# A two-layer hybrid trunk on one Trainium2 core: prologue in four quarters of channels, and five smaller edits

## The chip, the core and the metric

The kernel runs on one core of a Trainium2 chip. The engines are TensorE (PE; its weight loads are listed apart as PEld), VectorE (DVE), ScalarE (ACT), GpSimd (POOL) and SyncE (SP), which issues nearly all transfers. The metric is the device time of one execution in microseconds. TensorE has two clock levels, 1.2 and 2.4 GHz; the profile gives the granted clock as a share of full speed (0.50 and 1.00).

## What is computed

Two layers over 256 latent and 256 context tokens of width 1024, and a last norm of the latent tokens:

```python
for l in range(DEPTH):                                    # DEPTH = 2
    mod = silu_c @ mod_w[l] + mod_b[l]                    # 6 x 1024 values: shift, scale, gate, twice
    mod_c = silu_cc @ mod_w[l] + mod_b[l]
    ...
    h = rms_norm(x, norm_mix_g[l]) * (1.0 + sc1) + sh1    # the same for the context, with mod_c
    p = h @ w_in[l]
    # four mixers on column groups of p, in both directions: RG-LRU, RWKV-7, mLSTM, gated DeltaNet;
    # the context's final states start the latent tokens
    x = x + gt1 * (jnp.concatenate([ya, yb, yc, yd], axis=-1) @ w_out[l])
    h2 = rms_norm(x, norm_ffn_g[l]) * (1.0 + sc2) + sh2
    # layer 0: dense SwiGLU (2816 wide); layer 1: top 2 of 8 experts (1408 wide), latent tokens only
    y = swiglu(...) if l % 2 == 0 else moe_swiglu(...)
    x = x + gt2 * y
return rms_norm(x, final_norm_g)
```

## The kernel before

**Layout.** Activations lie as [128 channels x 512 tokens] tiles, eight to the width; columns 0 to 255 are context, 256 to 511 latent. Weights come from HBM as fp32 and are split on the fly by `wsplit` (lines 249 to 263): ACT casts a high part `whi` (L260), DVE subtracts to get the rest, `wlo` (L262). The normed activation is split in the same way into `hh` and `hl`. `mm3` then makes three matmuls of each product: hh by whi, hl by whi, hh by wlo. Nearly every matmul goes through the helper `mm` and shows line 246.

**Prologue** (`run`, lines 2157 to 2186). SP issues the constants `cst` (L197, 772 KB), the vectors of both layers (L200), the eight tiles of x (L2173), and 16 tiles `mw` of 512 KB with the modulation weights of shift and scale of layer 0's first norm. ACT and DVE add up the squares of x (`stat_add`, L376 to 380), `rms_rows` turns them into a row of factors `rs` in PSUM. `mod_block(0, j, True)` (L290 to 321) makes shift (j = 0) and scale (j = 1): 32 matmuls each with the two condition vectors as the 32-column stationary side, a copy to SBUF (`msb`), two transposes (L314), and the bias add into `mod`. Only then `norm` (L396 to 416) makes `nga` (gain times 1 + scale) and the eight normed tiles, and `inproj` (L419 to 446) starts.

**In-projection and loop.** The first group of `inproj` takes 4 output tiles at once, 8 weight tiles k by 12 matmuls, into two `pj` and two `pc` accumulators, and yields after each k. `mixers` (from L1495) runs a loop: each pass takes one step of the projection, and adds a credit to three lanes of mixer work and to the remaining `mod_block`s (in which the weights come in 256 KB tiles). The credits come from a table `PACE` by the number of the projection's step: for layer 0 (16, (1, .96, .6, 0)), then (29, (1.5, 2.4, .45, .5)), and so on to step 54. So the order on each engine follows from the count of yields. `rglru` (from L1430) multiplies by two 64x64 heads at a time, laid on the diagonal of a zero-filled 128x128 stationary tile `lruw`.

**Experts** (`moe_block`, from L1904). Pairs of experts gather their tokens by matmul with a one-hot tile `oh`: 8 tiles of PSUM, cast by ACT to `xgh` and `xgl` (L1960 to 1963). The way back uses the transposed `oht`; for the small experts the 64 rows of the upper and lower half are contracted apart (64 partitions). After the last pair `last_sums` (L1891 to 1902) squares each of the eight result tiles on ACT and sums it over channels by two matmuls with a column of ones (`lsq` in the profile).

**End of run.** All engines read the flag `big` (L2257). Under `tc.If(big > 0)` (L2260) stands the code for experts that overflow their first slots (`moe_rest`, not run with these inputs); `final` (L2129 to 2143) stands behind it.

Of the kernel before, what the change touches and what calls it, by code (L numbers as in the profile page):

```python
# [20 lines left out]
P = 128  # L21
# [44 lines left out]
COLMAP = _colmap()  # L66
T_WA, T_MISC, T_RKV, T_GDN, T_ML, T_LRU = 0, 1, 2, 8, 16, 24
# [20 lines left out]
def _consts():  # L88
# [16 lines left out]
    strict = np.stack([q[:, None] < i[None], q[:, None] > i[None]], 1)  # L105
    incl = np.stack([q[:, None] <= i[None], q[:, None] >= i[None]], 1)
    add("mstrict", strict)
    add("mincl", incl)
    add("id16", np.arange(32)[None, None, :] == 2 * np.arange(16)[None, :, None] + ((p % 32) // 16)[:, None, None])
    t = np.arange(T)  # L110
    rm = np.ones((P, T))
    for r in range(32):
        c = 128 if r < 4 else 64
        rm[r] = (t % c != 0)
        rm[32 + r] = (t % c != c - 1)
    add("rmask", rm)
# [31 lines left out]

def _negmasks():
# [5 lines left out]
    return np.concatenate([g.reshape(P, -1), m.reshape(P, -1)], 1).astype(np.float32)  # L155
# [27 lines left out]
class Trunk:  # L183
    def __init__(self, ctx, tc, t, dbg=None):
# [12 lines left out]
        nc.sync.dma_start(self.cst, t["cst"])  # L197
        self.pvt = [self.cp.tile([P, NPV], F32, name=f"pv{l}") for l in range(L)]
        for l in range(L):
            nc.sync.dma_start(self.pvt[l], t["pv"][l])  # L200
# [5 lines left out]
        nc.scalar.copy(self.identr, self.ident)  # L206

        self.pick = self.cp.tile([P, 2, 10, 64], F32R, name="pick")
        for d in range(2):
# [11 lines left out]
    def k(self, name):  # L221
        o, n = CSTN[name]
        return self.cst[:, o:o + n]
# [171 lines left out]
    def norm(self, l, gname, isc, ish, lo, rs, h32=None):  # L395
# [8 lines left out]
        for k in range(8):  # L404
            t = self.wk.tile([P, 512], F32, name=self.nm("nt"), tag="nt", bufs=3)
            nc.vector.tensor_tensor(t[:, lo:512], self.xT[:, k, lo:512], rs[:, lo:512], op=ALU.mult)  # L406
            for s in range(lo // 256, 2):
                o = t[:, 256 * s:256 * s + 256]
                ga, sh = gas[s][:, k:k + 1], self.modc(l, ish, s, k)
                if s == 0 and k % 2:  # L410
                    nc.vector.tensor_scalar(o, o, ga, sh, op0=ALU.mult, op1=ALU.add)
                else:
                    nc.scalar.activation(o if h32 is None else h32[:, k], o, AF.Identity, scale=ga, bias=sh)
            if h32 is None:
                nc.scalar.copy(self.hh[:, k, lo:512], t[:, lo:512])
                nc.vector.tensor_sub(self.hl[:, k, lo:512], t[:, lo:512], self.hh[:, k, lo:512].bitcast(F32))


    def inproj(self, l, tiles, evac, lat_only=()):  # L419
        if sorted(tiles[0:4]) == list(range(4)):  # L420
            pss = [self.pjt() for _ in range(2)] + [self.ps(), self.ps()]
            for k in range(8):
                wh, wl = self.wsplit(self.t["w_in0"][l, :, k], 4, P)
                for i in range(4):
                    tl, lo = tiles[i], 256 if i in lat_only else 0
                    self.mm3(pss[i][:, lo:512], wh[:, tl], wl[:, tl], self.hh[:, k, lo:512], self.hl[:, k, lo:512],
                             k == 0, k == 7)
                if k < 7:
                    yield
# [19 lines left out]
    def layer_params(self, l):  # L449
        nc = self.nc  # L450
        A = {}
        lw = self.cp.tile([P, 8, P], F32, name=f"lruw{l}", tag="lruw", bufs=1)
# [980 lines left out]
    def rglru(self, l, s, p, state, skip, new):  # L1433
# [64 lines left out]
    def mixers(self, l, xsrc, xdst):  # L1498
# [105 lines left out]
        def proj():  # L1604
            units = dict(rwkv=(0, [7, 6, 0, 1, 2, 3, 4, 5], ev_rwkv, (0, 1, 7), self.rwkv, ((), ())),
# [166 lines left out]
    def moe_route(self):  # L1772
# [20 lines left out]
        gt, eq = one("cgt", (P, 2, 8, 8)), one("ceq", (P, 2, 8, 8))  # L1793
# [97 lines left out]
    def last_sums(self, ms):  # L1891

        nc = self.nc
        for m in ms:
            if m == 0:
                self.lsum = self.ps2(0)
            sq = self.mp.tile([P, 256], F32, name=self.nm("lsq"), tag="hs", bufs=2)
            nc.scalar.activation(sq, self.xT[:, m, 256:512], AF.Square)
            for b in range(2):
                self.mm(self.lsum[:, b, 0:1], sq[:, 128 * b:128 * b + 128], self.one, m == 0, m == 7)  # L1900
            if m == 7:
                nc.vector.tensor_copy(self.ssq, self.lsum[:, :, 0])

    def moe_block(self, ids, cols, small, place, gate, off, last=False):  # L1904
# [8 lines left out]
        if off:  # L1913
            io = T_("ceq", (P, 128), 1)
            nc.vector.tensor_scalar(io, iota, float(off), None, op0=ALU.add)
            iota = io
# [15 lines left out]
        def gather(p):  # L1932
# [16 lines left out]
            for k in range(8):  # L1949
                ps = self.ps()  # L1950
                ohc = lambda b, o, n: cat(oh, 256 * b + o, [[1, n]])
                tk = lambda i, b: (self.tokh, self.tokl)[i][:, b, 128 * k:128 * k + 128]
                for b in range(2):
                    self.mm(ps[:, 0:n], tk(0, b), ohc(b, 0, n), b == 0, b == 1 and not half)
# [440 lines left out]
```

## Time and profile before

| | us |
|---|---|
| median of 3 runs (lowest, highest) | 1874.96 (1871.52, 1887.96) |
| the profiled execution | 1870.76 |
| its span | 1869.0 |
| prologue and the first group of layer 0 (up to 66 us) | 66 |
| rest of layer 0's mixers (66 to 560 us) | 494 |
| dense feed-forward of layer 0 (560 to 940 us) | 380 |
| mixers of layer 1 and router (940 to 1440 us) | 500 |
| experts (1440 to 1843 us) | 403 |
| sums and last norm (from 1843 us) | 26 |

The stages were cut where the lines of the program change. The table of windows gives, per stage, TensorE's busy time and its granted clock; a stage in which the engine is nearly always busy can only get shorter by fewer or faster matmuls, one in which it idles by what it waits for.

### The profile page before, as it was taken

To read this page: it belongs to the slowest core of one execution; us is meant where nothing else is said; L and a number is where in the kernel's file an instruction comes from. 1 tells how busy PE (TensorE), PEld (TensorE's weight loads), DVE (VectorE), ACT (ScalarE), POOL (GpSimd) and SP (SyncE) were. 2 spreads that over 40 slices of the span, in tenths; PEclk is the share of its full clock that TensorE was granted. 3 is DMA by queue.
4 is the path that set the end of the run, shared out by engine and by line. 5 is a ranking of instruction groups with operands and counts; after the bars stand their busy time and mean duration, and the time that the engine had idled before them with its cause. 6 is when DMAs were issued, how large, how long until landed. Compare 5 with 4: busy or idle time off the path is not lost. (4 is left out here: it accounts for less than half of the span.)

```text
span 1869.0 us, 31932 instructions
## 1 busy us (share of the span) xinstructions
PE 1695.7 (91%) x12340; PEld 1301.5 (70%) x12340; DVE 1106.6 (59%) x2414; ACT 901.3 (48%) x1655; POOL 33.5 (2%) x88
## 2 busy tenths in 40 slices
PE   5989988997996999999979899899787999999996
PEld 2767666774784888888867576587676888666663
DVE  5577368778566333333356657787755887364542
ACT  4554464775534333332245545568434776344431
POOL 0000001000000000000000000000000000000000
PEclk8979897998997999999989799899785999999997
DMA  7433343144443333333334344421233998897992
GB/s 283 149 102 130 123 130 108 60 144 162 143 132 101 98 96 96 96 96 96 99 116 149 110 146 159 151 83 62 65 105 124 395 359 286 314 400 291 403 346 118
DMA packets 124002, 309.60 MB, mean 166 GB/s; under 512 B 13440, under 2 KB 39296, under 8 KB 111424
## 3 DMA queue, kind: packets, MB, share of 16 engines
q1 hardware_dynamic: 123840, 307.46, 47.7%
q8 instruction: 99, 1.62, 0.4%
q14 instruction: 63, 0.52, 0.1%
HBM read 286.77 MB, written 20.64 MB: 164 GB/s over the span
## 5 line engine op out<-in xcount | busy, mean ns | idle before, releaser
L262 DVE TENSOR_TENSOR wlo<-w,whi 128x512 fp32r<-128x512 f32 (+3 forms) x386 | 381.4, 993 | 319.7 <-ACT whi L260 305.0
L260 ACT CAST whi<-w 128x512 fp32r<-128x512 f32 (+3 forms) x386 | 332.3, 865 | 397.8 <-PE pj L246 146.1
L246 PE MATMUL pj<-hh,whi 128*128 128x512 f32 (+1 forms) x544 | 225.2, 415 | 29.1 <-ACT whi L260 15.1
L246 PE MATMUL pj<-hh,wlo 128*128 128x512 f32 (+1 forms) x544 | 220.3, 406 | 4.4 <-DVE wlo L262 4.2
L246 PE MATMUL pj<-hl,whi 128*128 128x512 f32 (+1 forms) x544 | 216.8, 399 | 0.4 <-DVE hl L1291 0.2
L246 PEld LDWEIGHTS pj<-hh,whi 128*128 128x128 f32 x544 | 113.1, 208 | 56.9 <-ACT whi L260 19.4
L246 PE MATMUL pj<-mw,sc 128*32 128x256 f32 x768 | 104.0, 428 | 45.4 <-DMA mw<-in_mod_w 45.2
L246 PEld LDWEIGHTS pj<-hh,wlo 128*128 128x128 f32 x544 | 113.3, 208 | 33.9 <-DVE wlo L262 10.1
L246 PEld LDWEIGHTS pj<-hl,whi 128*128 128x128 f32 x544 | 113.7, 209 | 17.6 <-DVE hl L1291 0.9
L246 PE MATMUL pm<-wlo,xgh 128*128 128x512 f32 (+1 forms) x240 | 93.2, 388 | 1.4 <-DVE wlo L262 1.4
L246 PE MATMUL pm<-whi,xgh 128*128 128x512 f32 (+1 forms) x240 | 92.7, 388 | 0.0
L246 PE MATMUL pm<-whi,xgl 128*128 128x512 f32 (+1 forms) x240 | 91.6, 382 | 0.0
L246 PEld LDWEIGHTS pj<-mw,sc 128*32 128x32 f32 x768 | 27.6, 116 | 87.0 <-DMA mw<-in_mod_w 44.4
L246 PE MATMUL pj<-fh,whi 128*128 128x512 f32 x176 | 68.7, 390 | 0.0
L246 PE MATMUL pj<-fh,wlo 128*128 128x512 f32 x176 | 68.6, 390 | 0.0
L246 PE MATMUL pj<-fl,whi 128*128 128x512 f32 x176 | 68.5, 389 | 0.0
L246 PE MATMUL pm<-hh,whi 128*128 128x512 f32 x160 | 62.3, 390 | 0.0
L246 PE MATMUL pm<-hl,whi 128*128 128x512 f32 x160 | 62.3, 389 | 0.0
L246 PE MATMUL pm<-hh,wlo 128*128 128x512 f32 x160 | 62.3, 389 | 0.0
L246 PE MATMUL pm<-w,xgs 128*64 128x192 f32 (+1 forms) x384 | 60.7, 462 | 0.0
L246 PE MATMUL pc<-hh,whi 128*128 128x512 f32 (+1 forms) x128 | 49.6, 387 | 7.5 <-DVE nt L406 4.0
L246 PEld LDWEIGHTS pm<-wlo,xgh 128*128 128x128 f32 x240 | 46.4, 193 | 10.6 <-DVE wlo L262 3.3
(658 smaller groups left out, 3407.2 us busy)
## 6 DMA issues: line engine op xcount, KB each, us to landing
w<-in_moe_gu SPq DMA_DIRECT2D x64, 1024.0 KB, 7.1
mw<-in_mod_w SPq DMA_DIRECT2D x160, 256.0 KB, 3.0
w<-in_moe_d SPq DMA_DIRECT2D x32, 1024.0 KB, 7.6
w<-in_w_in SPq DMA_DIRECT2D x112, 256.0 KB, 2.9
w<-in_moe_gv SPq DMA_DIRECT2D x32, 768.0 KB, 6.2
w<-in_ffn_gu SPq DMA_DIRECT2D x88, 256.0 KB, 2.7
w<-in_moe_d SPq DMA_DIRECT2D x16, 768.0 KB, 6.4
pp<-pd SPq DMA_DIRECT2D x46, 256.0 KB, 3.5
```

Source lines behind the costliest of these rows:

```text
L246: self.nc.tensor.matmul(out, lhsT, rhs, start=start, stop=stop)
L260: nc.scalar.copy(hi, w)
L262: nc.vector.tensor_sub(lo, w, hi.bitcast(F32))
```

## The change

1. **Prologue by quarters.** `first_norm` makes shift and scale for 256 channels at a time: 32 matmuls of 128 columns, one copy (`mqs`), one transpose, bias add and `nga` for two tiles, the norm of these two tiles, and the first group's matmuls for these two k (`inproj_first`). The same 8 MB of modulation weights come in 8 transfers of 1 MB. The first group's accumulators are two `pj` and the two halves of a `pm` pair. `cst` is smaller (266 KB) and is issued behind four of the tiles of x. The first group no longer yields in layer 0, so that the loop has 7 steps fewer before it; `PACE` stays.
2. **Compact masks.** The four masks move from `cst` to `cstm` (192 KB before, 720 KB now) and are kept as bf16 (`maskb`). `lruw` holds 64 columns instead of 128 (no zeros), and `rglru` makes two 64x64 matmuls where it made one of 128x128.
3. **Paired gather.** Four pairs of PSUM tiles (`pm`), with casts of twice the size, in place of eight single ones.
4. **128-row ways back.** A small expert's `oht` is split into two tiles with 64 zero rows each (POOL clears them), and the way back contracts over 128 rows.
5. **Paired squares.** Two squares are added on DVE before the sum, so that `lsq` has 8 matmuls instead of 16, issued one tile later.
6. **Last norm inside the branch.** `If(big < 1)` holds `final` as the way that falls through; `Else` holds the overflow code and a `final` of its own.

```diff
+    def constants(self):
+        nc = self.nc
         nc.scalar.copy(self.identr, self.ident)
+        nc.vector.tensor_copy(self.identb, self.ident)
...
+    def first_norm(self):
+        nc = self.nc
+        rs = None
+        tiles = [self.WTILE[i] for i in RWKV_TILES[0:4]]
+        ps2 = self.ps2(0)
+        self.begun = [self.pjt(), self.pjt(), ps2[:, 0], ps2[:, 1]]
+        m, o = self.modt[0], PVN["modb"][0]
+        gas = [self.sm((P, 8), "nga", 2) for _ in range(2)]
+        for q in range(4):
+            w = [self.wk.tile([P, 4, 512], F32, name=self.nm("mq"), tag="mq", bufs=8) for _ in range(2)]
+            for i in range(2):
+                nc.sync.dma_start(w[i], self.t["mod_q"][q, :, 4 * i:4 * i + 4])
+            if rs is None:
+                rs = self.rms_rows(0)
+            pm = self.ps2(1)
+            for k in range(8):
+                for g in range(4):
+                    self.mm(pm[32 * g:32 * g + 32, 0, 0:128], self.sc[:, k, :], w[k // 4][:, k % 4, 128 * g:128 * g + 128],
+                            k == 0, k == 7)
+            sb = self.wk.tile([P, 128], F32, name=self.nm("mqs"), tag="mqs", bufs=2)
+            nc.vector.tensor_copy(sb, pm[:, 0, 0:128])
+            nc.tensor.transpose(pm[:, 1, 0:128], sb, self.ident)
+            nc.vector.tensor_tensor(cat(m, 4 * q, [[16, 2], [2, 2], [1, 2]]), cat(pm, 512, [[64, 2], [32, 2], [1, 2]]),
+                                    cat(self.pvt[0], o + 2 * q, [[8, 2], [1, 2], [0, 2]]), op=ALU.add)
+            ks = range(2 * q, 2 * q + 2)
+            for s in range(2):
+                nc.vector.scalar_tensor_tensor(gas[s][:, 2 * q:2 * q + 2], cat(m, 16 + 4 * q + s, [[2, 2]]), 1.0,
+                                               self.pv(0, "nmg", 2 * q, 2), op0=ALU.add, op1=ALU.mult)
+            for k in ks:
+                self.norm_tile(0, 0, 0, rs, gas, k)
+            for k in ks:
+                self.inproj_first(0, tiles, (), self.begun, k)
...
     def inproj(self, l, tiles, evac, lat_only=()):
         if sorted(tiles[0:4]) == list(range(4)):
...
+            pss, self.begun = self.begun, None
+            if pss is None:
+                pss = [self.pjt() for _ in range(2)] + [self.ps(), self.ps()]
+                for k in range(8):
+                    self.inproj_first(l, tiles, lat_only, pss, k)
+                    if k < 7:
+                        yield
...
-                self.mm(pp[:, 0, c], A["lruw"][:, 4 * d + j], u[:, j])
-                self.mm(pp[:, 1, c], A["lruw"][:, 4 * d + 2 + j], u[:, j])
+                for g in range(2):
+                    for h in (slice(0, 64), slice(64, 128)):
+                        self.mm(pp[h, g, c], A["lruw"][h, 4 * d + 2 * g + j], u[h, j])
...
+    def last_squares(self, m):
...
+        for h in range(2):
+            nc.scalar.activation(sq[:, h], self.xT[:, m + 4 * h, 256:512], AF.Square)
+        nc.vector.tensor_tensor(sq[:, 0], sq[:, 0], sq[:, 1], op=ALU.add)
...
-            for k in range(8):
-                ps = self.ps()
+            for k2 in range(0, 8, 2):
+                ps = self.ps2()
...
+                nc.scalar.copy(xh[:, k2:k2 + 2, 0:m], ps[:, :, 0:m])
+                nc.scalar.copy(xl[:, k2:k2 + 2, 0:m], ps[:, :, 256:256 + m])
...
+                if small[e]:
+
+                    oht[e] = [T_("oht", (P, 256), 6, F32R) for _ in range(2)]
+                    for h in range(2):
+                        nc.gpsimd.memset(oht[e][h][H_[1 - h]].bitcast(F32), 0.0)
+                        nc.scalar.copy(v2(oht[e][h])[H_[h]], way[H_[h]])
...
         for k in range(8):
+            if k == 4:
+                nc.sync.dma_start(self.cst, self.t["cst"])
+                nc.sync.dma_start(self.pvt[0], self.t["pv"][0])
             nc.sync.dma_start(self.xT[:, k], self.t["x_t"][:, k])
             self.stat_add(k, 0)
...
+        self.constants()
+        self.first_norm()
+        nc.sync.dma_start(self.pvt[1], self.t["pv"][1])
         cm = self.ptile("cstm", (P, CSTM.shape[1]))
...
+        nc.vector.tensor_copy(self.maskb, cm[:, 384:])
...
-        with tc.If(big > 0):
+        with tc.If(big < 1) as here:
+            self.final()
+        with here.Else():
             self.moe_rest()
-            self.last_sums(range(8))
-        self.final()
+            for m in range(4):
+                self.last_squares(m)
+                self.last_sums(m)
+            self.final()
```

What the change moves on the engines is shown at three places. A row is a line of the program, the operation, output <- inputs, and the shape; numbers behind a name tell tiles of one name apart.

The first is TensorE between the modulation and the first group. Before, `mw` are modulation weights, `msb` the copied result, `hh` and `hl` the normed activation:

```order
L246 MATMUL pj_235<-mw_278,sc 32x256 x4
L314 MATMUL pj_286<-cst,msb_284 128x128 x2
L246 MATMUL pj_411<-hh,whi_416 128x512
L246 MATMUL pj_411<-hl,whi_416 128x512
L246 MATMUL pj_412<-hh,whi_416 128x512
```

And in the changed kernel, from the end of the first quarter's matmuls to the start of the second's (`mq` are modulation weights, `mqs` the copied result, pm_280 the second quarter's accumulator, pm_371 the third's):

```order
L264 MATMUL pm_145<-hh,wlo_260 128x512
L264 MATMUL pm_280<-mq_276,sc 32x128 x7
L264 MATMUL pm_280<-mq_277,sc 32x128 x16
L463 MATMUL pm_280<-cst,mqs_313 128x128
L264 MATMUL pm_371<-mq_367,sc 32x128 x16
L264 MATMUL pj_146<-hh,whi_332 128x512
L264 MATMUL pj_147<-hh,whi_332 128x512
```

The modulation of the second quarter, 23 of its matmuls and the transpose, stands behind all of the first quarter's projection; the third and fourth quarter's transposes stand in the same way behind the k tiles of the quarter before.

The second place is VectorE ahead of the last quarter (`maskb` and its neighbours are the masks, `wlo` a split weight, `mod` and `nga` the last quarter's modulation, `lmz` and `lmq` small constants of a mixer):

```order
L438 TENSOR_TENSOR hl<-nt_416,hh 128x512
L462 COPY mqs_495<-pm_462 128x128
L428 TENSOR_TENSOR nt_507<-xT_89,pc_180 128x512
...
L2259 CAST gmaskb<-cstm_550 128x128
L2260 CAST mmaskb<-cstm_550 128x256
L2261 CAST maskb<-cstm_550 128x1024
L280 TENSOR_TENSOR wlo_515<-w_513,whi_514 128x512
...
L464 TENSOR_TENSOR mod_101<-pm_462,pv_70 128x2x4
L468 SCALAR_TENSOR_TENSOR nga_148<-mod_101,pv_70 128x2
```

The casts of the masks, which wait for the transfer of `cstm`, now stand ahead of the last quarter's `mod`; before, the first stood ahead of the second half's copy `msb` and the second behind it, both ahead of the norm.

The third is TensorE at the end. Before (`oht` the way back, `lsq` the squares; the rows behind the branch are the overflow code):

```order
L246 MATMUL pc_16886<-oht_16095,hh 128x256 x2
L246 MATMUL pm_16844<-cst,lsq_16881 128x1 x2
L246 MATMUL pm_16844<-cst,lsq_16893 128x1 x2
L246 MATMUL pm_16844<-cst,lsq_16897 128x1 x2
L2257 TENSOR_LOAD bigi
L2260 COMPARE_AND_BRANCH
L246 MATMUL pc_16921<-oh_16914,hl 128x256 x4
```

And in the changed kernel:

```order
L264 MATMUL pc_16930<-oht_16092,hh 128x256 x2
L264 MATMUL pm_16906<-cst,lsq_16925 128x1 x2
L264 MATMUL pm_16906<-cst,lsq_16939 128x1 x2
L2335 TENSOR_LOAD bigi
L2338 COMPARE_AND_BRANCH
L264 MATMUL pc_16968<-identr,pth_16964 128x128
```

The sum's matmuls are half as many, and directly behind the branch stand the matmuls of the last norm, in which `pth` is the high part of the norm's factors.

## Rows read from the trace of the kernel before

**Rows 1.** The page: busy time, share of the span and instructions of two engines
```profile
PE 1695.7 (91%) x12340; PEld 1301.5 (70%) x12340; DVE 1106.6 (59%) x2414; ACT 901.3 (48%) x1655; POOL 33.5 (2%) x88
```

**Rows 2.** Windows by stage, TensorE: window, length, busy (records), clock, DMA share, GB/s
```profile
0.00:66.00 66.00, 42.83 (x244) 0.90 0.64 237
66.00:560.00 494.00, 454.78 (x4290) 0.90 0.39 126
...
1440.00:1843.00 403.00, 388.11 (x1961) 0.97 0.88 339
1843.00:1869.00 26.00, 11.61 (x52) 0.58 0.12 44
```

**Rows 3.** Timeline of the prologue: start, duration, engine, line, tiles, [idle before <- releaser]
```profile
21.22 1.88 DVE L406 TENSOR_TENSOR nt<-xT,pc 128x512 f32<-128x512 f32 x3 [1.86 <-PE pc L246]
...
26.12 1.50 PE L246 MATMUL pj<-mw,sc 128*32 128x256 f32 x24
...
33.54 1.08 PE L246 MATMUL pj<-mw,sc 128*32 128x256 f32 x8 [0.16 <-DMA mw<-in_mod_w]
...
34.69 0.42 DVE L311 COPY msb<-pj 128x256 f32<-128x256 f32 x1 [0.48 <-PE pj L246]
...
36.30 1.58 ACT L413 ACTIVATE nt<-nt,mod,nga 128x256 f32<-128x256 f32 x3 [17.14 <-DVE nga L402]
...
38.82 1.09 ACT L413 ACTIVATE nt<-nt,mod,nga 128x256 f32<-128x256 f32 x2
...
40.32 0.61 ACT L415 CAST hh<-nt 128x512 fp32r<-128x512 f32 x1
...
40.47 0.79 PE L246 MATMUL pj<-hh,whi 128*128 128x512 f32 x1 [4.61 <-ACT whi L260]
...
41.76 0.69 DVE L262 TENSOR_TENSOR wlo<-w,whi 128x512 fp32r<-128x512 f32 x1
```

**Rows 4.** Timeline, near the end of the first group
```profile
59.78 0.39 PE L246 MATMUL pj<-hl,whi 128*128 128x512 f32 x1
...
64.76 0.39 PE L246 MATMUL pc<-hh,wlo 128*128 128x512 f32 x1
```

**Rows 5.** Windows of 2 us, TensorE, columns as in rows 2
```profile
30.00:32.00 2.00, 0.64 (x8) 0.87 1.02 404
32.00:34.00 2.00, 1.54 (x16) 0.50 1.02 404
...
44.00:46.00 2.00, 2.00 (x8) 0.72 0.22 73
...
66.00:68.00 2.00, 0.90 (x4) 1.00 0.00 0
```

**Rows 6.** Waits of TensorE, 66 to 560 us: us in total, times, longest
```profile
PE pj L246 <- DMA mw<-in_mod_w: 19.4, 16, 3.1
```

**Rows 7.** Groups by shape, whole span: records | busy us, mean ns | idle before, releasers
```profile
L246 PE MATMUL pm<-w,xgs 128*64 128x512 f32 x192 | 44.0, 594 | 0.0
...
L246 PE MATMUL pm<-pp,lruw 128*128 128x256 f32 x64 | 18.3, 413 | 1.6 <-ACT dmb L1452 1.3 <-ACT dgf L1190 0.2
L246 PE MATMUL pc<-oht,hh 128*128 128x256 f32 x80 | 16.9, 314 | 3.9 <-DVE xT L1993 3.5 <-ACT hth L2096 0.4
L246 PE MATMUL pc<-oht,hh 64*128 64x256 f32 x48 | 12.8, 377 | 2.7 <-ACT hh L2101 1.7 <-DVE xT L1993 0.6
```

**Rows 8.** Timeline of the first gather of experts
```profile
1443.76 0.37 ACT L1960 CAST xgh<-pc 128x256 fp32r<-128x256 f32 x1 [1.36 <-PE pc L246]
```

**Rows 9.** Timeline of the end: last squares and sums, branch, last norm
```profile
1844.99 0.61 PE L246 MATMUL pm<-cst,lsq 128*128 128x1 f32 x4
...
1851.55 2.72 PE L246 MATMUL pm<-cst,lsq 128*128 128x1 f32 x12
...
1854.30 0.16 DVE L1902 COPY ssq<-pm 128x2 f32<-128x2 f32 x1 [2.16 <-PE pm L246]
1858.65 0.17 DVE L343 TENSOR_SCALAR rq<-ssq 128x2 f32<-128x2 f32 x1 [4.19 <-DVEq L2260]
```

More of the change, by code (lines that the diff above doesn't have):

```diff
@@ L146, with _masks @@
 CST = _consts()
+MSKN = {}
+def _masks():
+    cols, off = [], 0
+    p = np.arange(P)
+    q, i = p % 64, np.arange(64)
+    t = np.arange(T)
+    rm = np.ones((P, T))
+    for r in range(32):
+        c = 128 if r < 4 else 64
+        rm[r] = (t % c != 0)
+        rm[32 + r] = (t % c != c - 1)
+    for name, a in (("mstrict", np.stack([q[:, None] < i[None], q[:, None] > i[None]], 1)),
+                    ("mincl", np.stack([q[:, None] <= i[None], q[:, None] >= i[None]], 1)),
+                    ("id16", np.arange(32)[None, None, :] == 2 * np.arange(16)[None, :, None] + ((p % 32) // 16)[:, None, None]),
+                    ("rmask", rm)):
+        a = np.asarray(a, np.float32).reshape(P, -1)
+        MSKN[name] = (off, a.shape[1])
+        cols.append(a)
+        off += a.shape[1]
+    return np.concatenate(cols, 1)
 def _negmasks():
@@ L404, in norm @@
         for k in range(8):
[L405 to L413, printed above, removed]
@@ L419, in inproj, with inproj_first @@
+    def inproj_first(self, l, tiles, lat_only, pss, k):
+        wh, wl = self.wsplit(self.t["w_in0"][l, :, k], 4, P)
+        for i in range(4):
+            tl, lo = tiles[i], 256 if i in lat_only else 0
+            self.mm3(pss[i][:, lo:512], wh[:, tl], wl[:, tl], self.hh[:, k, lo:512], self.hl[:, k, lo:512],
+                     k == 0, k == 7)
     def inproj(self, l, tiles, evac, lat_only=()):
         if sorted(tiles[0:4]) == list(range(4)):
-            pss = [self.pjt() for _ in range(2)] + [self.ps(), self.ps()]
@@ L451, in layer_params @@
         A = {}
-        lw = self.cp.tile([P, 8, P], F32, name=f"lruw{l}", tag="lruw", bufs=1)
+        lw = self.cp.tile([P, 8, 64], F32, name=f"lruw{l}", tag="lruw", bufs=1)
         nc.sync.dma_start(lw, self.t["lru_w"][l])
@@ L1889, in moe_main, with last_sums @@
         self.moe_block([ids[s] for s in order], order, [s >= FULL for s in order], self.slot, self.slotg, 0, True)
-    def last_sums(self, ms):
+    def last_squares(self, m):
         nc = self.nc
[L1894 to L1902, printed above, removed]
+        sq = self.mp.tile([P, 2, 256], F32, name=self.nm("lsq"), tag="hs", bufs=2)
+        for h in range(2):
+            nc.scalar.activation(sq[:, h], self.xT[:, m + 4 * h, 256:512], AF.Square)
+        nc.vector.tensor_tensor(sq[:, 0], sq[:, 0], sq[:, 1], op=ALU.add)
+        self.lsq = sq
+    def last_sums(self, m):
+        if m == 0:
+            self.lsum = self.ps2(0)
+        for b in range(2):
+            self.mm(self.lsum[:, b, 0:1], self.lsq[:, 0, 128 * b:128 * b + 128], self.one, m == 0, m == 3)
+        if m == 3:
+            self.nc.vector.tensor_copy(self.ssq, self.lsum[:, :, 0])
     def moe_block(self, ids, cols, small, place, gate, off, last=False):
@@ L1981, in back @@
                 ps = [self.ps(), self.ps()]
[L1982 to L1990 removed]
+                for h in range(2):
+                    for i, e in enumerate(es):
+                        c = 128 * (m if small[e] else m + 4 * h)
+                        for q in range(2):
+                            self.mm(ps[h][:, 0:256], ys[e][q][:, c:c + 128], oht[e][h], i + q == 0, i == len(es) - 1 and q == 1)
+                if sums and m:
+                    self.last_sums(m - 1)
                 for h in range(2):
```

110 lines of the change are left out of this document (46 added, 64 removed).

## The prediction

> **What bounds the kernel now.** I read the page first, then the windows by stage, then the timeline where a stage idles. TensorE is busy for 91% of the span, DVE for 59% [rows 1], so what counts is TensorE's own time and what it waits for. The windows [rows 2] part the span. From 66 to 560 us it idles for 494.00 - 454.78 = 39.2 us, at a granted clock of 0.90; in the experts it is busy for 388.11 of 403 us at 0.97; in the prologue it idles for 23.2 of 66 us, and in the tail for 14.4 of 26 us. The last two are what the change mainly addresses: at most 38 us, 2% of the time.
>
> The prologue in order [rows 3]: from 21.22 the norm's products `nt` are made, and wait; the last modulation matmuls run at 33.54 behind the last `mw` transfer; then comes a chain without cover, the copy at 34.69, the scaling at 36.30, and the first projection matmul at 40.47. The group then runs to about 65.15 (64.76 + 0.39) [rows 4]: 24.7 us for its 96 matmuls. The clock stands at half speed by 33 us and comes back at about 45 us [rows 5]: at 0.72 over 44 to 46 us, about 0.9 of these 2 us ran at full speed. So the group's first 4.6 us ran at half speed, which lost 2.3 us.
>
> **The prologue by quarters.** TensorE executes its rows in order, and the order listed above puts the rest of quarter q's modulation behind the projection of quarter q-1. So the quarters don't overlap; each pays a chain in the open.
>
> - Start. Ahead of x stand 506 KB of constants less (and one `pv`). At the 404 GB/s of a window in which transfers ran without a pause [rows 5] the 506 KB are 1.25 us; with the second `pv` I take 1.7 us (0 to 3), so `nt` starts at 19.5 instead of 21.22. Three products 1.9 [rows 3]: 21.4. From the copy to the scaling the old chain took 36.30 - 34.69 = 1.6: 23.0. Two `wlo` of 0.69 now stand between on DVE: 24.4. Two scalings 1.1 and the cast of `hh` 0.6 [rows 3]: the first matmul is at 26.1 instead of 40.47. The first quarter's modulation has its data well before: 2 MB at 404 GB/s are 5.2 us.
> - Group. Its own 24.7 us stay.
> - Second quarter in the open: 23 modulation matmuls of 128 columns. With 256 columns one took 1.50/24 = 0.063 at full and 1.08/8 = 0.135 at half clock [rows 3]; 23 are 1.4 to 3.1, I take 2.0. Then 1.6 + 1.1 + 0.6 and a handover, 3.4. Sum 5.4.
> - Third: 15 matmuls (0.9 to 2.0, I take 1.2) and 3.4: 4.6. The matmuls issued ahead for the quarter after lie in the chain's shadow.
> - Fourth: its modulation is complete, only its transpose stands behind k tile 5; without the copy, 3.1.
> - The casts of the masks ahead of the last `mod` on DVE wait for `cstm`. It is asked for behind the weights of k tile 7, which need a buffer that k tile 4 frees, around 43 us by these sums; 720 KB then take 1.8 us at 404 GB/s. The last quarter's chain starts near 54: covered by 9 us. Without that cover it would be late by what the transfer is late.
>
> Sum: 26.1 + 24.7 + 5.4 + 4.6 + 3.1 = 63.9, against 65.15: -1.2. On the other side stands the clock. The chains are pauses; around a 2-us pause at 66 us it stayed at full speed, in the gappy 30 to 34 us it fell [rows 5]. Three pauses of 3.1 to 5.4 lie between, so zero to three falls of about 2.3 each: 0 to 6.9, I take one. The old group's 24.7 holds one cold start already. **Prologue +1.1** (-5 to +5).
>
> **Layer 0's order.** Seven steps of the loop vanish, the table of credits stays: lanes start about 3.5 projection steps later against the projection, the modulation blocks 7. No instruction is added. TensorE's 39.2 us of idle and the half-clock stretches can be dealt out anew; 16 waits for `mw` alone make 19.4 us [rows 6]. A gain is possible since those blocks now meet later steps, a loss since they crowd into fewer. Nothing in the rows decides it; bound by about a third of the idle time either way, 12 us. I take **-3** (-12 to +12), towards gain because seven weight tiles less are shared with the lanes.
>
> **rglru.** 64 records of 128x128 by 256 columns take 18.3 us [rows 7]; they become twice as many of a quarter of the array. If the two quadrants run beside each other the time stays, if they run one after the other it doubles: 0 to +18. The nearest row is `w` by `xgs`: two column halves of 512 columns take 44.0/192 = 0.229 each [rows 7], less than a record of 256 columns takes in `lruw` (0.286). So halves there run beside each other, and I take **+1**. The Trainium skill, "TensorEngine Tiling (Array Packing)", Key Properties, says two things: tiles work in parallel, which this row bears out, but a change of the tiling mode drains the array, which no row here prices; by the first the sum stays, by the second it would rise a little.
>
> **Experts.** Ways back: 48 records of 64 rows take 12.8/48 = 0.267, those of 128 rows 16.9/80 = 0.211 [rows 7]; as many, so at most 48 x 0.056 = 2.7 us less, of which I take 2, since some of it is waiting. The added clears (POOL) and casts are hidden by the expert's own matmuls. Paired gather: TensorE is nearly gapless here, so fewer casts gain nothing; but the gather now takes the accumulators of the first expert, whose matmuls must wait for the last casts. Each cast is 0.37 [rows 8]; four to eight of them are 1.5 to 3; the first gather has it open, others less: +1. **-1** (-4 to +3).
>
> **Tail** [rows 9]. Sums: `lsq` matmuls took 0.15 (4 in 0.61) at full and 0.23 (12 in 2.72) at half clock. Eight fewer are 1.2 to 1.9; squares no longer alternate with the ways back: **-2** (-3 to 0). Branch: DVE idles 4.19 us between the sum (1854.30) and the last norm (1858.65), released by its own sequencer at the branch. Falling through should save part of it; the read of the flag stays. I take half, **-2** (-3.5 to 0). [...]
>
> **Sum.** +1.1 - 3 + 1 - 1 - 4 = -5.9. Against the profiled execution's 1870.76 that is 1864.9, **1865 us**. This execution lies 4 us below the median of the runs, 1874.96, and 0.8 below the lowest; I keep to it, since undisturbed executions lie close together.
>
> **The rivals.**
>
> *B, the quarters overlap.* If each quarter's chain lay beside the projection of the one before, the 13.1 us in the open would go: the prologue would give -14.3 (and no clock lost), the rest stays at -7: 1849.5 us. For it: the modulation's data come at full rate, TensorE idle 23 us. Against it: the order listed, in which the transposes stand behind the projection, and an in-order engine. Chance 0.13.
>
> *C, slower: waits for modulation weights in layer 0.* They are 16 waits with 19.4 us, 1.21 each [rows 6], of 96 loads (6 blocks of 16). If the later start bunches them so that 40 of 96 wait, that is 48.5, +29: 1864.9 + 29 = 1893.9. It decides from 21 more waits on (1% over). For it: the blocks get the same credit in fewer steps, and share the transfer queue with projection weights that come faster. Against it: transfers there move 126 GB/s [rows 2], far from the 404. Chance 0.12, of which 0.09 over 1%.
>
> *D, quadrants one after the other.* Each pair of `lruw` matmuls serial: +18 instead of +1, less what lies under a DVE-bound stretch, some 2: 1864.9 + 15 = 1880. For it: the pair shares the moving data's columns and writes one PSUM bank. Against it: the row of `xgs`. Chance 0.13.
>
> **How the numbers follow.** My forecast has 0.62, with its own range 1853 to 1878 (the root of the squared half-ranges 5, 12, 3.5 and 3 is 14, and less for 8 in 10). About 1% is what a measurement of this kernel can tell from no change: 1856.2 and 1893.7 around the median, and taken against the profiled execution 1852 and 1889. Faster: B (0.13), and the lower end of the forecast (0.11): 0.24. Slower: C 0.09. Same: 0.67. The range for 8 in 10 reaches from 1846, which takes in B, to 1888, which takes in D and leaves out C.
>
> **What would show it.** Each quarter: the first `hh` by `whi` matmul near 26 and the last of k tile 7 near 64 to 66; three pauses before k tiles 2, 4, 6; the granted clock in them. If the last stands near 51, B holds. Layer 0: idle time of TensorE up to the feed-forward and its waits for `mw`. `lruw`: busy time of its records near 18, not 36. Tail: DVE's idle ahead of `rq` near 2 instead of 4.19. I am wrong above all if the new order of layer 0 moves more than 12 us either way, since this term is a guess about an order and the others are sums of rows.

## The result: 1852.3 us, faster by 1.1%

The changed kernel takes 1852.3 us in the median of 13 runs (1850.46 to 1867.38), the kernel before 1874.34 in its 13. The ratio is 0.9886, with a 95% interval of 0.9868 to 0.9905. I had forecast 1865 and "within 1%" as the likeliest, with 0.24 for faster by more than that. The time lies inside the range for 8 in 10 (1846 to 1888) and just below the forecast's own (1853 to 1878); it moved clearly, and further than I said. That 1865 is so near owes something to its start: it was counted from the profiled execution, 1870.76, and not from the median, 3.6 higher. Between the medians 22.0 us went, where 5.9 were forecast.

The profiled execution has a span of 1849.1 instead of 1869.0. On the page TensorE's busy time answers [rows 1] with 24.4 us less, although it has more instructions:

```profile
PE 1671.3 (90%) x12516; PEld 1284.3 (69%) x12516; DVE 1105.9 (60%) x2430; ACT 897.7 (49%) x1613; POOL 35.4 (2%) x94
```

To see where the time went, I cut both traces at the same instructions: the end of the first group, the first and the last down-projection matmul of the dense feed-forward, the first gather matmul, the last down-projection matmul of the experts. The windows of the changed kernel, TensorE alone (window, length, busy with records, granted clock, DMA share, GB/s; they answer [rows 2]); the first two lines are layer 0 and the experts of the kernel before, cut in this way:

```profile
65.15:835.70 770.55, 713.15 (x5403) 0.92 0.37 116
1442.50:1841.90 399.40, 387.54 (x1961) 0.98 0.89 342
...
0.00:66.18 66.18, 43.03 (x372) 0.92 0.63 230
66.18:826.60 760.42, 698.80 (x5434) 0.96 0.38 118
826.60:945.80 119.20, 119.19 (x527) 1.00 0.35 97
945.80:1430.10 484.30, 422.32 (x4190) 0.87 0.36 115
1430.10:1824.90 394.80, 379.82 (x1961) 0.98 0.90 346
1824.90:1849.10 24.20, 8.09 (x40) 0.63 0.13 47
```

| stage | before, us | after, us | change | forecast |
|---|---|---|---|---|
| prologue and first group | 65.2 | 66.2 | +1.0 | +1.1 |
| layer 0, to the first down-projection | 770.6 | 760.4 | -10.1 | -3 (-12 to +12), and a share of rglru |
| dense down-projection | 119.2 | 119.2 | 0 | 0 |
| layer 1's mixers and router | 487.6 | 484.3 | -3.3 | a share of rglru's +1 |
| experts | 399.4 | 394.8 | -4.6 | -1 (-4 to +3) |
| sums and last norm | 27.1 | 24.2 | -2.9 | -4 |
| sum | 1869.0 | 1849.1 | -19.9 | -5.9 |

In layer 0 the gain is not idle time. TensorE idles 770.55 - 713.15 = 57.4 us there before and 61.6 after, four more. Its busy time fell from 713.15 to 698.80 at a few more records, with the granted clock at 0.96 instead of 0.92. The same work ran at the higher level more of the time.

### The profile page after: what moved, and what is told of

It is laid out like the page before. It is cut to its first block, busy times and chain, and to the rows that moved or that the text cites. A ratio compares the mean times of both kernels' runs of the same rounds, so it can differ in the third digit from the quotient of the medians.

```text
span 1849.1 us, 32265 instructions
## 1 busy us (share of the span) xinstructions
PE 1671.3 (90%) x12516; PEld 1284.3 (69%) x12516; DVE 1105.9 (60%) x2430; ACT 897.7 (49%) x1613; POOL 35.4 (2%) x94
## 4 chain that ended last, share of the span: by engine, by line
PE 72%; DVE 10%; ACT 9%; DMA 6%; issue 2%; SPq 0%; DVEq 0%; ACTq 0%
PE pm L264 26%; PE pj L264 24%; PE pc L264 12%; PE pd L264 5%; PE pf L264 3%; DMA mw<-in_mod_w 3%; DVE wlo L280 1%; DMA w<-in_moe_d 1%; ACT whi L278 1%; DVE dma L1526 1%; ACT nt L435 1%; ACT dri L796 0%; ACT dge L796 0%; DVE nt L428 0%; DMA xo<-pst 0%
## 5 line engine op out<-in xcount | busy, mean ns | idle before, releaser
L264 PEld LDWEIGHTS pj<-hh,whi 128*128 128x128 f32 x544 | 110.8, 205 | 66.2 <-ACT whi L278 20.5
L264 PE MATMUL pj<-mw,sc 128*32 128x256 f32 x640 | 93.5, 397 | 16.4 <-DMA mw<-in_mod_w 16.2
L264 PE MATMUL pm<-hl,whi 128*128 128x512 f32 x176 | 69.4, 394 | 0.0
L264 PE MATMUL pm<-hh,wlo 128*128 128x512 f32 x176 | 69.2, 393 | 0.0
L264 PE MATMUL pm<-hh,whi 128*128 128x512 f32 x176 | 69.2, 393 | 0.0
L264 PEld LDWEIGHTS pj<-mw,sc 128*32 128x32 f32 x640 | 23.7, 109 | 50.7 <-DMA mw<-in_mod_w 26.2
L264 PE MATMUL pm<-w,xgs 128*64 128x512 f32 (+1 forms) x384 | 58.6, 461 | 0.0
L264 PEld LDWEIGHTS pm<-whi,xgh 128*128 128x128 f32 x240 | 45.6, 190 | 7.1
```

What stands on the lines that cost most here:

```text
L264: self.nc.tensor.matmul(out, lhsT, rhs, start=start, stop=stop)
```

## The experiments

In all of them the stage lengths come from the same cuts, and the medians from runs beside runs of the kernel before on the same chip.

### The changed kernel again

Nothing edited.

> The changed kernel itself, beside the next three on one chip, since executions differ by some us. Theory S (layer 0's order and the granted clock in it set the difference): its executions spread with the granted clock, layer 0 stays 8 to 12 us below that of the kernel before, and the experts stay within 1 us of 394.8, since nothing in them depends on the clock of layer 0. Time about 1852. A rival, that the 10 us of layer 0 were one lucky execution, expects layer 0 near 770 and about 1862.

Median 1853.69 (1845.73 to 1858.58, 4 runs), ratio 0.9859 (0.9811 to 0.9908). Layer 0 took 761.5, layer 1 482.4, the experts 395.7, the tail 24.9:

```profile
65.55:827.00 761.45, 704.60 (x5435) 0.95 0.36 117
```

So layer 0's gain is there again, and the rival of one lucky execution falls. The four runs go roughly with their clocks: 1845.73 at 0.938, 1851.03 at 0.932, 1856.34 at 0.927, 1858.58 at 0.928.

### Where layer 0's gain comes from: four edits of the order

First, the seven steps put back, as empty ones behind the first group.

```diff
             if pss is None:
...
+            else:
+                for k in range(7):
+                    yield
```

> The changed kernel with seven empty steps put back into layer 0's loop ahead of the second group, so that the table of credits meets the same steps as before; no other instruction differs. Theory S (the 10 us that layer 0 gained come from the shifted order of lanes and modulation blocks, which leaves less of TensorE's work at half clock): layer 0 from the end of the first group to the first down-projection matmul gets 8 to 12 us longer again, its mean granted clock falls from 0.94 to about 0.90, time about 1861. Theory W (they come from lighter work: bf16 masks, smaller rglru weights, less competing transfers): within 2 us of the changed kernel's 1852.

Median 1867.58 (1857.45 to 1879.02, 10 runs), ratio 0.9977 (0.9946 to 1.0009): the gain is gone, though the prologue, the gather, the ways back and the branch are those of the changed kernel. Layer 0 of the profiled execution:

```profile
65.98:846.00 780.02, 720.73 (x5434) 0.91 0.35 114
```

It is even longer than before the change (770.6), 7.6 of the 9.5 us in busy time, and 19.6 longer than in the changed kernel, where I had expected 8 to 12; this execution, 1873.51, is above the median. The median is 5.5 us below the kernel before on the same chip, where the changed kernel's two are 22.0 and 21.9 below: 16 us are lost again. TensorE's waits for modulation weights in 66 to 560 us are back too (total, times, longest), against 7.4 in 13 in the changed kernel:

```profile
PE pj L264 <- DMA mw<-in_mod_w: 21.5, 16, 3.2
```

Second, the reverse: the kernel before, without the seven steps and with nothing else.

```diff
-                if k < 7:
+                if k < 7 and l:
                     yield
```

> The kernel before, with nothing changed but that the first group of layer 0 no longer yields, so that the loop has seven steps fewer. Theory S: this alone brings most of layer 0's gain: 8 to 20 us less between the end of the first group and the first down-projection matmul, granted clock 0.94 to 0.96 there instead of 0.92, waits for modulation weights below 10 us instead of 19.4, time 1855 to 1865. Theory W (lighter masks and weights): no change, 1873.

```profile
65.44:826.00 760.56, 703.47 (x5402) 0.95 0.36 118
```

Layer 0 falls to 760.6, that of the changed kernel, with old masks, old rglru, old prologue. The median is 1867.82 (1860.86 to 1877.60, 10 runs), ratio 0.9955 (0.9929 to 0.9980): 7.7 us below the kernel before in the median, where I had expected 1855 to 1865; the profiled execution, 1860.97, is one of its shortest. Theory S holds in its direction, with a size between 7.7 (taking the steps out) and 16 us (putting them back), and theory W falls. The loop's step count, a side effect of the edit, is the largest single term.

Third and fourth: is it the lanes or the modulation blocks? Each alone is put back to the projection steps at which it ran before.

```diff
+            if l == 0:
+                at = lambda j: next((p for e, p in self.PACE[0] if j < e), self.PACE[0][-1][1])
+                pace = (*at(max(n + 0, 0))[0:3], at(max(n + 7, 0))[3])
             n += 1
```

That is the kernel with the modulation blocks put back; the other, with the lanes put back, has the 7 in the first place and the 0 in the second.

> The changed kernel, with the modulation blocks of layer 0 alone put back to the projection steps at which they ran before (their rate is looked up seven steps further on); the lanes keep the new order. Theory M (the gain of layer 0 comes from the later modulation blocks: their waits for weights come at a place where TensorE has little else queued and the clock falls with them): first narrow modulation matmul near 97 to 105 us instead of 148, waits for its weights back to 15 to 22 us, clock of layer 0 0.91 to 0.93, layer 0 770 to 780, time 1860 to 1868. Theory N (the lanes' shift makes it): layer 0 stays near 761, time near 1853.

> The changed kernel, with the rates of the three mixer lanes of layer 0 looked up seven steps further on, as they stood against the projection before; the modulation blocks keep the new, later place. Theory M: layer 0 stays near 761 (758 to 766), waits for modulation weights below 10 us, time 1850 to 1856. Theory N: layer 0 770 to 780, time 1860 to 1868.

With the old place of the modulation blocks the median is 1868.79 (1865.74 to 1873.70, 10 runs), with the old place of the lanes 1853.54 (1853.20 to 1859.17, 4 runs). Layer 0 of the first:

```profile
67.66:842.90 775.24, 708.84 (x5436) 0.93 0.35 115
```

and of the second:

```profile
66.81:830.00 763.19, 706.94 (x5435) 0.94 0.35 117
```

By the times theory M holds, though 1868.79 is just above its 1860 to 1868: moving the blocks from 148 us back to 98.8 costs the whole gain, and moving the lanes costs nothing that can be measured. Its mechanism does not hold. With the blocks at the old place TensorE idles 775.24 - 708.84 = 66.4 us, and is busy for 708.84; against the changed kernel's two profiles (61.6 and 56.9 idle, 698.80 and 704.60 busy) both parts grow, and the waits for modulation weights come to 12.7 us, fewer than the 15 to 22 that I expected.

In the kernel before, the first modulation matmuls stand among other small ones, with a pause between them. From a timeline of TensorE:

```profile
97.03 1.06 PE L246 MATMUL pj<-mw,sc 128*32 128x256 f32 x12
...
101.16 0.63 PE L246 MATMUL pc<-cst,sgd 64*64 64x4 f32 x16
103.11 1.87 PE L246 MATMUL pc<-cst,sge 64*64 64x4 f32 x32 [1.31 <-DVE sge L649]
```

The clock falls within this group, at about 103 us, and stays at half until about 117 us, while the projection's wide matmuls run again. With the blocks alone put back there, it doesn't fall. TensorE around that place and at the end of the mixers, in the kernel before:

```profile
97.00:116.00 19.00, 16.83 (x123) 0.66 0.30 98
543.00:574.00 31.00, 25.12 (x103) 0.89 0.55 172
```

and with the blocks put back:

```profile
97.00:116.00 19.00, 18.92 (x163) 1.00 0.45 155
543.00:574.00 31.00, 18.35 (x65) 0.50 0.10 32
```

So this kernel loses elsewhere. Its last modulation matmul runs at 487.8 us instead of 525.6, and from 538 to 569 us TensorE has little besides small matmuls of the last lanes, waits once for 6.8 us for one of their tiles (`srd`), and runs at half clock; in the changed kernel other work lies beside those lanes. The two edits therefore don't part what made the order of the kernel before slow: that the whole shift of seven steps is worth 8 to 16 us is shown, which part of it, and which matmuls or waits bring the clock down, is not.

### Single gather

The eight gather tiles of before, in place of four pairs.

```diff
-            for k2 in range(0, 8, 2):
-                ps = self.ps2()
+            for k in range(8):
+                ps = self.ps()
...
```

> The changed kernel with the eight single gather tiles of before. Theory G (pairing costs the first expert's start and is worth nothing in a TensorE-bound stretch): the first expert's matmul comes about 5 us sooner after the first gather's start, the experts as a whole 0 to 2 us shorter, 1850 to 1852. Theory H (pairing is what made the experts 4.6 us shorter, by fewer waits for casts): experts 3 to 5 us longer, 1855 to 1857.

```profile
1435.50:1830.30 394.80, 381.07 (x1959) 0.99 0.89 346
```

The experts take 394.8, as with pairs (394.8 and 395.7). The first expert starts 3.8 us behind the first gather instead of 9.2, and all of that is made up later. Pairing is worth nothing in this stage either way. The median, 1855.38 (1852.96 to 1858.50, 4 runs), is the number of theory H, but not by its reason: in the profiled execution the experts take no more time than with pairs, and layer 1, which this edit doesn't touch, takes more (489.4).

### 64-row ways back

```diff
-                if small[e]:
-                    oht[e] = [T_("oht", (P, 256), 6, F32R) for _ in range(2)]
...
+                oht[e] = T_("oht", (P, 256), 4, F32R)
...
+                    if small[e]:
+                        todo += [(h, H_[h], q, m, e) for q in range(2) for h in range(2)]
```

> The changed kernel with the 64-row ways back of before. Theory R (the 4.6 us that the experts lost are the 128-row ways back, not the gather, which was worth nothing): experts 3 to 5 us longer, 398 to 399.5, the time about 1856. Theory N (a full 128-row contraction costs as much as two 64-row ones beside each other, and the gain lies elsewhere): experts stay at 394.8 within 1 us.

The experts take 400.1, just above theory R's 398 to 399.5, and the median is 1857.03 (1853.00 to 1864.44, 4 runs). Two parts are to be seen. The records themselves: 17.4 us (80 of 128 rows) and 8.4 (32 of 64 rows) against 22.1 for the 112 of the changed kernel, so 3.7 us. And the clock behind them. Timeline and clock windows of this kernel, from the second of the stage's two ways back that begin with 64-row blocks:

```profile
1739.04 0.90 PE L264 MATMUL pc<-oht,hh 64*128 64x256 f32 x4 [0.56 <-ACT hh L2173]
1740.52 1.80 PE L264 MATMUL pc<-oht,hh 128*128 128x256 f32 x8 [0.57 <-DVE xT L2063]
...
1746.12 0.63 PE L264 MATMUL pm<-whi,xgh 128*128 128x512 f32 x1
```

```profile
1741.00:1742.50 1.50, 1.50 (x8) 0.91 1.00 415
1742.50:1744.00 1.50, 1.50 (x4) 0.50 1.01 421
...
1747.00:1748.50 1.50, 1.50 (x5) 0.50 1.01 415
```

and of the changed kernel at the same place:

```profile
1731.17 0.93 PE L264 MATMUL pc<-oht,hh 128*128 128x256 f32 x4 [0.66 <-ACT hh L2177]
1732.56 1.52 PE L264 MATMUL pc<-oht,hh 128*128 128x256 f32 x8 [0.46 <-DVE xT L2067]
...
1737.42 0.40 PE L264 MATMUL pm<-whi,xgh 128*128 128x512 f32 x1
```

```profile
1732.00:1733.50 1.50, 1.00 (x6) 1.00 1.05 437
1733.50:1735.00 1.50, 1.23 (x8) 1.00 1.01 421
...
1736.50:1738.00 1.50, 1.14 (x5) 1.00 1.01 421
```

Behind the 64-row block the clock fell to half, and the next expert's matmuls took 0.63 instead of 0.40 until about 1749; behind the 128-row block it stayed full, although TensorE paused more there. The 20-us window that holds this place stood at 0.83 in all three profiles with 64 rows (before, this one, and the one of before without the seven steps) and at 1.00 in all eleven with 128 rows.

But the rows alone don't decide it. At the first of the two ways back, some 100 us earlier, the clock of the changed kernel fell behind the same matmuls with 128 rows:

```profile
1635.28 1.60 PE L264 MATMUL pc<-oht,hh 128*128 128x256 f32 x8 [0.46 <-DVE xT L2067]
...
1641.11 0.63 PE L264 MATMUL pm<-wlo,xgh 128*128 128x512 f32 x1
```

The 20-us window there stood at 0.83 in the three profiles with 64 rows, and at 0.83 or 0.91 in the eleven with 128. So the wider form went with one fall instead of two at these ways back; why the other stays is open.

### Old tail

Single squares, and the last norm behind the branch.

```diff
...
-        with tc.If(big < 1) as here:
-            self.final()
-        with here.Else():
+        with tc.If(big > 0):
             self.moe_rest()
-            for m in range(4):
-                self.last_squares(m)
-                self.last_sums(m)
-            self.final()
+            self.last_sums(range(8))
+        self.final()
```

> The changed kernel with the single squares and the last norm behind the branch, as before. If the two tail edits are worth what the tail lost in all (2.9 us), the stretch from the last down-projection matmul to the end goes from 24.2 to about 27; by the forecast's sizes 2 of it stand ahead of the branch and 2 at it: DVE's idle ahead of the first step of the last norm goes from 1.2 back to 4.2. Time 1855 to 1857.

Median 1853.51 (1852.25 to 1855.88, 4 runs), tail 24.7: between the 24.2 and 24.9 of the changed kernel, where I had expected about 27 and 1855 to 1857. Both tail edits together are worth nothing that can be told apart from the spread of executions, although the branch does what it should. The changed kernel, DVE from the sum to the last norm (answers [rows 9]):

```profile
1834.40 0.16 DVE L1971 COPY ssq<-pm 128x2 f32<-128x2 f32 x1 [1.38 <-PE pm L264]
1835.76 0.17 DVE L361 TENSOR_SCALAR rq<-ssq 128x2 f32<-128x2 f32 x1 [1.20 <-issue]
```

and this one:

```profile
1835.70 0.16 DVE L1966 COPY ssq<-pm 128x2 f32<-128x2 f32 x1 [1.87 <-PE pm L264]
1840.07 0.17 DVE L361 TENSOR_SCALAR rq<-ssq 128x2 f32<-128x2 f32 x1 [4.21 <-DVEq L2329]
```

At the branch 4.37 - 1.36 = 3.0 us go. They come back at the end. The tail in four pieces, from the timelines:

| us | last expert matmul to sum | sum to norm | norm to last output tile | last output tile to end |
|---|---|---|---|---|
| before | 11.8 | 4.4 | 6.3 | 4.0 |
| changed | 8.9 | 1.4 | 6.4 | 7.0 |
| old tail | 9.3 | 4.4 | 6.3 | 4.1 |
| 64-row ways back | 10.9 | 1.4 | 6.4 | 6.8 |

In the changed kernel the engines jump over `Else` at the end, while the outputs are written. In its last 11 us the queues that carry instructions made nine transfers (transfers, MB, share), and an output tile took 3.7 us in the median to land:

```profile
q14 instruction: 7, 0.06, 1.8%
q8 instruction: 2, 0.03, 1.5%
...
out<-fy SPq DMA_DIRECT2D x4, 256.0 KB, 3.7
```

With the old tail there were two, and 2.6 us:

```profile
q8 instruction: 1, 0.02, 0.5%
q14 instruction: 1, 0.01, 0.2%
...
out<-fy SPq DMA_DIRECT2D x4, 256.0 KB, 2.6
```

The 3.7 us are those of one execution: the other profiles with this branch had 2.9 to 3.8. That the fetches hold up the outputs on the same DMA engines is how I read it; a kernel with the jump and without the fetches wasn't tried. It is also only part of the 3.0 us: with the old tail the kernel ended 1.4 us behind the landing of the last output tile, in the changed kernel's two profiles 2.3 and 2.9 us behind it. The table also suggests what shortened the tail: not the squares (9.3 to 8.9, and 9.5 in the changed kernel's second profile) but the 128-row ways back of its last experts (10.9 to 8.9).

### rglru on the whole array

```diff
...
-                for g in range(2):
-                    for h in (slice(0, 64), slice(64, 128)):
-                        self.mm(pp[h, g, c], A["lruw"][h, 4 * d + 2 * g + j], u[h, j])
+                self.mm(pp[:, 0, c], A["lruw"][:, 4 * d + j], u[:, j])
+                self.mm(pp[:, 1, c], A["lruw"][:, 4 * d + 2 + j], u[:, j])
```

> The changed kernel with the zero-filled 128x128 weights of rglru. Theory Q (quadrants run beside each other): TensorE's busy time of these records goes from 20.6 back to about 18, the time stays within 3 us of 1852, and layer 1 from the last down-projection matmul to the first gather stays near 484. Theory L (layer 1's 3.2 us come from the quadrant form): layer 1 gets about 3 us longer.

```profile
L264 PE MATMUL pm<-pp,lruw 128*128 128x256 f32 x64 | 20.5, 455 | 1.1 <-ACT dgc L1204 0.9 <-ACT dgf L1252 0.2
```

And the quadrants of the changed kernel, and of the overlapped kernel below in its second run:

```profile
L264 PE MATMUL pm<-pp,lruw 64*64 64x256 f32 x128 | 20.6, 422 | 1.7 <-ACT dgc L1204 1.4 <-ACT dgf L1252 0.2
L264 PE MATMUL pm<-pp,lruw 64*64 64x256 f32 x128 | 24.6, 492 | 1.8 <-ACT dgc L1207 1.4 <-ACT dgf L1255 0.3
```

The changed kernel's 128 quadrant records took 20.6 us, the 64 whole ones here 20.5. Over all profiles quadrants took 19.1 to 24.6 us (eleven) and whole ones 18.3 to 20.5 (three). So quadrants run beside each other, far from a doubling, and may cost a few us more. In the time even the sign is open: the median, 1859.25 (1854.38 to 1860.11, 5 runs), is above the 1849 to 1855 that I expected of theory Q, and layer 1 at 488.0 is theory L's 3 us longer, with layer 0 at 762.9. But layer 1 lay anywhere from 481.7 to 489.4 in kernels that agree in it, so neither this nor the -3.3 between before and after can be told from that spread.

### The quarters overlapped

In the prologue, the modulation and norm of quarter q+1 are written ahead of the projection of quarter q.

```diff
-            for k in ks:
-                self.inproj_first(0, tiles, (), self.begun, k)
+            if q:
+                for k in (2 * q - 2, 2 * q - 1):
+                    self.inproj_first(0, tiles, (), self.begun, k)
+        for k in (6, 7):
+            self.inproj_first(0, tiles, (), self.begun, k)
```

> The changed kernel with the code order of the prologue shifted by one quarter: modulation, transpose and norm of quarter q+1 stand ahead of the projection of quarter q. If the exposed chains are what keeps the prologue at 66 us (the forecast's working), the first group ends at 53 to 57 instead of 66.2 and the time falls by about 10, to 1842, unless layer 0's later order gives some of it back. If the quarters are held by the transfers instead, it ends at 62 or later and the time stays near 1850.

> The prologue shifted by one quarter, again, beside the others, since its executions lay between 1839.5 and 1856. First group ends near 56, as before; by the prologue's 10 us alone 1842 to 1844, with executions spread by the clock of layer 0 (0.92 to 0.95) over some 10 us.

The first group ends at 56.0 (first time) and 57.5 (second) instead of 66.2. The medians are 1845.01 (1839.52 to 1855.97, 4 runs) and 1842.82 (1840.42 to 1848.78, 6 runs, ratio 0.9820, 0.9797 to 0.9844): faster than both kernels. Layer 0 of the two profiled executions:

```profile
55.95:831.70 775.75, 718.63 (x5435) 0.92 0.35 115
```

```profile
57.51:819.70 762.19, 704.92 (x5434) 0.94 0.36 117
```

This is one program, with 3.6 and 3.8 us of waits for modulation weights and 57.1 and 57.3 of idle time in all: 13.6 us of difference lie in busy time at another clock. So a single profile of layer 0 says little, and the judgments above rest on medians as well.

Last, the same with the modulation blocks three steps later still.

```diff
...
+                pace = (*at(max(n + 0, 0))[0:3], at(max(n + -3, 0))[3])
...
```

> The prologue shifted by one quarter, and layer 0's modulation blocks three steps later still. If later blocks go on cutting the waits and half-clock stretches, layer 0 is 2 to 5 us shorter than in the next kernel, time 1838 to 1842. If the gain of the later place is used up, it stands within 2 us of the next, or above it, because the blocks then delay the end of layer 0.

Median 1866.66 (1858.13 to 1871.21, 8 runs): 24 us worse than without, far more than I had allowed for.

```profile
56.73:836.40 779.67, 709.93 (x5436) 0.93 0.35 115
```

Idle time is 69.7 us, waits for modulation weights 12.6, and the blocks' last matmul runs at 552.7 us instead of 518.2, so the blocks now delay the end of the layer. "Later is better" isn't the rule either: seven steps later gained, ten lost it again.

## Why the prediction was right or wrong

**Prologue: right, nearly to the number.** The first matmul was forecast at 26.1, the group's end at 63.9 without and about 66.2 with one fall of the clock. The changed kernel's TensorE, at the first `hh` by `whi` matmuls of the four quarters and the last of the group:

```profile
26.45 1.22 PE L264 MATMUL pj<-hh,whi 128*128 128x512 f32 x2 [1.95 <-ACT hh L437]
...
39.71 0.72 PE L264 MATMUL pj<-hh,whi 128*128 128x512 f32 x2 [1.24 <-ACT hh L437]
...
50.32 0.73 PE L264 MATMUL pj<-hh,whi 128*128 128x512 f32 x2 [0.36 <-ACT hh L437]
...
58.79 0.73 PE L264 MATMUL pj<-hh,whi 128*128 128x512 f32 x2 [2.58 <-ACT hh L437]
...
65.79 0.39 PE L264 MATMUL pm<-hh,wlo 128*128 128x512 f32 x1
```

The projections of the quarters before ended at 34.96, 46.01 and 56.10, so the open chains took 4.8, 4.3 and 2.7, forecast 5.4, 4.6 and 3.1. After the last the next matmuls took 0.63 instead of 0.39: the one fall. That the end is so near is in part luck: the chains came to 11.8 us instead of 13.1, while the start was 0.35 late, and the rest, 27.9 us, exceeded 24.7 + 2.3 by 0.9. Rival B, overlap, failed for the reason given, the order on TensorE; the overlapped kernel shows that this order, and not the transfers, was what held it.

**Layer 0's order: the step that failed.** I wrote that nothing in the rows decides it and took -3 of +-12. It was -10.1 in the profile, 7.7 in the median when the steps alone were taken out, and 16 when they alone were put back. The sign was right; the bound held for two of these three. The size was a guess: of the 14.0 us by which the profile came out below the forecast, 7.1 are this term. I had counted idle time (39.2 us up to 560) as what could be won; the gain was in busy time at the granted clock (713.15 to 698.80 us, idle time 57.4 to 61.6), which I bounded for the prologue and not here, though [rows 2] showed 0.90 for 494 us. Rival C looked at the modulation blocks and their waits, with the wrong sign: the waits fell from 19.4 to 7.4. The blocks of the old order start at 97 us, those of the new one at 148; which part of the shift moved the clock stays open.

**rglru: right on TensorE, not settled in the time.** 20.6 us against 20.5 for the whole form, 19.1 to 24.6 over all profiles: near 18, not 36, and rival D falls. The drain at a change of tiling mode that the Trainium skill names ("TensorEngine Tiling (Array Packing)", Key Properties) can't be told from the records' spread.

**Experts: right that the gather gains nothing, wrong on the ways back.** I took 2 for them and 1 against for the gather. Undoing the ways back cost 4.4 to 5.3 us in the experts and 1 to 2 in the tail; the gather's late first start was made up. The step counted the records' own time, up to 2.7 (3.7 were measured), and no clock. The Trainium skill, "TensorE: Matmul & The Clock Gate", HAM oscillation — how this bites in real kernels, explains falls of the clock by waits for transfers. The trace agrees only in part: none of the waits shown at these falls is for a transfer, and the second place had a fall with 64-row matmuls and none with 128 rows and longer pauses.

**Tail: right sum, by luck.** -2.9 against -4. The squares gave 0.4 us at most instead of 2 (their upper bound, 8 x 0.227, is also 1.8 and not 1.9). The branch gave 3.0 at its entrance, where I took 2, and cost 3.0 at its exit. What the tail gained in all came from the ways back, which this sum didn't hold. The Trainium skill ("Runtime: NRT & Kernel Launch", Instruction fetch mechanics) says that a taken branch whose target is outside the window of fetched code has to wait for a fetch. The trace agrees as far as the nine transfers of instructions at the exit go. My step looked at the entrance and not at the jump that the way that falls through needs at its end.

**What stays open.** Layer 1's 3.3 us, the bf16 masks alone (not tried), and what exactly makes the clock fall in layer 0 and in the experts: the order decides it in layer 0, waits for modulation weights alone don't, and executions of one program differ by 10 us and more.

## What to carry to other kernels

An edit that changes the number of steps in a hand-paced loop moves everything that is paced by it; test that side effect by itself, since here it was worth more than any of the edits. Splitting it further can mislead: a kernel with half of the old order back was as slow as before, but in another place, so compare the stretches and not only the sums. Where TensorE is busy but its granted clock lies below 1, price the clock like a stall: look at what stands just ahead of a fall, and try the same work in another place or form. The fall-through branch here, which ends in a jump, moved its price of 3.0 us and didn't remove it.

## What the runs showed of the hardware that I had not expected

- Behind one way back with 64-row matmuls the clock stood at 0.50 for some 6 us, and behind the same product with 128 rows, zeros included, at 1.00; at another way back 100 us earlier it fell with both.
- One program, two executions, 775.8 and 762.2 us in the same stage, with equal idle time (57.1 and 57.3 us) and clocks of 0.92 and 0.94.
- Two 64x64 quadrants take about as long as one 128x128 matmul with zeros: 19.1 to 24.6 us in all against 18.3 to 20.5.
- Transfers of instructions at a jump (nine instead of two) go with slower output transfers: 2.9 to 3.8 us instead of 2.6 for 256 KB.
